# Branch 3 of the dilated attention in whole tiles of q, k, exchanged q and v, loaded two residues ahead, its outputs in one tile of 15 slots, and two weight blocks loaded over a shorter stretch

## The chip, the cores and the metric

One core of a Trainium2 chip runs the whole program. The metric is device time in microseconds, the median of several executions. The core's engines work through queues of their own, in order: PE (TensorE, the matrix products), ACT (ScalarE), DVE (VectorE), POOL (GpSimd) and SP (SyncE), which here issues nearly all transfers (DMAs). An instruction waits on semaphores for what others make; whatever stands behind it on its engine waits with it.

## The reference

The kernel computes one step of a one-layer hybrid decoder on a prompt of 2048 positions and 64 sample rows (8 sequences of 8 new positions on a cache). A normed input is projected once into q, k, v of an attention, qb, kb, vb of a gated linear attention (GLA), its low-rank gate, and two output gates. The attention has three branches of (window, dilation); their outputs are mixed by their softmax denominators. GLA runs over chunks of 64. Both results are gated and go through one output projection:

```
DILATED = ((128, 1), (512, 4), (2048, 16))

def dilated_branch_prompt(q, k, v, window, dil):
    n_keys = window // dil + 1
    lm = S // dil
    ...
    valid = (dist >= 0) & (dist < n_keys) & (key_m >= 0)
    s = jnp.einsum('brnqhd,brnkhd->brnqhk', qr, kk) * (hd ** -0.5)
    s = jnp.where(valid[None, None, :, :, None, :], s, -jnp.inf)
    o, lse = softmax_attend(s, vv, 'brnqhk,brnkhd->brnqhd')
```

Branch 3 has dilation 16: the positions fall into 16 residues of 128 positions each, and each residue is a causal attention of 128 queries on 128 keys, for 8 heads of width 64.

## The kernel before, in words

The program has three parts in time. In the first, up to about 480 us, the projections v, q and k run over 16 row tiles of 128 positions. In the second, up to about 730 us, the attention runs, woven with the projection qkb (qb and kb together). In the third GLA runs, woven with the projections g (gates), vb (value gates) and gb; at the end come the mixing and the output projection (Y, L1658).

**Projections.** `project` (L1107) multiplies in f16 with every number split into a high and a low half: 24 matmuls for one row tile and one block (L1127), with `hr`/`hl` as weights of the array. Their sums are called acc_qkb, acc_g, acc_vb, acc_gb. They need no result of the attention, and so serve as filler between its matmuls. Weights come in through a chain, `load_w`: per block 8 loads from DRAM (`wr_`, L601), a pass of squares on ACT (`jw_`, L622), and a scaling into the two halves on ACT (L649) and DVE (L650).

**Attention.** Branches 1 and 2 run in units (`unit`, L829), then branch 3 (`branch3`, L912): 16 residues r, each in two halves a of four heads, 32 sub-items in all. A sub-item has four stages: `pre` (the loads), `qk` (L444: scores s of high and low halves; DVE adds the mask and takes the row's limit, L452; ACT takes the exponential, L455), `tr` (PE transposes p, L462; ACT with DVE, L424 and L425, or ACT twice and POOL, L427 to L429, split it into halves pt) and `pv` (L477: the output O; ACT and DVE add its halves, L493 and L494; SP stores it, L937). `pipeline` (L1074) staggers them: in one round come qk of sub-item n, pre of n+1, pv of n-3 and tr of n-1.

For the scores, branch 3 needs the query tile twice: as loaded, with the high halves in 64 partitions and the low ones in the other 64, and with the two exchanged. `exchanged` (L815) makes the second with two DVE copies (L818). `turned3` loads the transposed q and k of a residue (L909), one residue ahead; `pre` loads v (L925). Their tiles lie in the pool b3, with two buffers for each of Tq (as loaded and exchanged side by side), Tk and v3. The outputs o lie in the pool op with seven buffers, which the units share.

**Order.** `weave` (L358) interleaves generators: at each point it advances the one whose share done, (steps + 0.5) / declared steps, is smallest. L1218 weaves the rest of qkb, the attention, the weight chain of g and vb (declared 4 x KT = 32 steps, where it has 34 yields) and the sample attention's dots. A scheduler then fixes the order of instructions on each engine from its own estimate of their times; the tile framework adds the waits. A DMA on SP takes one of eight semaphores in turn, DMAHW0 to DMAHW7, and waits for the one issued eight before it.

**GLA.** Its pools (L1224) are opened after the attention's pools are closed, and take over their memory. What lies on a tile's place must have been read, or its store landed, before the new tile is written. Eight cores of 256 positions (`gla_core`, L143) each load zqk and zg (L155, L161), transpose the gates (pg, L190), build decays and scores (sc, L281) and end with the transposes ptk (L324).

Of the kernel before, what the change touches and what calls it, by code (L numbers as in the profile page):

```python
# [7 lines left out]
F32 = mybir.dt.float32  # L8
F32R = mybir.dt.float32r
F16 = mybir.dt.float16  # L10
# [8 lines left out]
P = 128  # L19
D = 1024  # L20
KT = D // P
NH = 8
# [30 lines left out]
def tile_hymba(ctx: ExitStack, tc: tile.TileContext, A: dict):  # L53
    nc = tc.nc
    PE, ACT, DVE, POOL, SP = nc.tensor, nc.scalar, nc.vector, nc.gpsimd, nc.sync
# [20 lines left out]
    o3_d = scratch("o3_d", S, 528)  # L76
# [4 lines left out]
    kp_d = dram.tile([S, 2 * NH * HD], F16, name="kp_d")  # L81
    qp_d = dram.tile([S, 2 * NH * HD], F16, name="qp_d")
    vp_d = dram.tile([S, 2 * NH * HD], F16, name="vp_d")
# [263 lines left out]
    def by16(ap, r):  # L347
        return ap.rearrange("(i r) c -> r i c", r=16)[r]
# [3 lines left out]
    def chain(*gens):  # L352
        for g in gens:
            yield from g
# [3 lines left out]
    def weave(*parts, until=()):  # L358

        until = list(until or parts)
        parts = list(parts)
        for p in parts:
            p.append(0)
        while any(any(q is p for p in parts) for q in until):
            for p in sorted(parts, key=lambda p: (p[2] + 0.5) / p[1]):
                r = next(p[0], parts)
                if r is not WAIT:
                    break  # L370
            p[2] += 1
            if r is parts:
                parts = [q for q in parts if q is not p]
        return [[g, n - done] for g, n, done in parts]
# [7 lines left out]
    with ExitStack() as c1:  # L382
# [22 lines left out]
        op = c_att.enter_context(tc.tile_pool(name="op", bufs=7))  # L405
        ap_ = c_att.enter_context(tc.tile_pool(name="ap", bufs=2))
# [182 lines left out]
        def load_w(name, between=(), behind=()):  # L589

            if name in ("o0", "o1"):
                src, c0, n, rows, sh = w_out, 512 * int(name[1]), 512, nwo, 1.0
            else:
                src, (c0, n), rows, sh = w_in, BLOCKS[name], nw, H_SCALE
            raws = []
            mx = sm.tile([P, KT], F32, name=f"wm_{name}", tag="wm")
            for k in range(KT):
                if k % 2 == 0:
                    pair = wr.tile([P, 2, 528], F32, name=f"wr_{name}_{k}", tag="wr")
                raw = pair[:, k % 2]  # L600
                SP.dma_start(raw[:, :n], src[k * P : (k + 1) * P, c0 : c0 + n])  # L601
                raws.append(raw)
                if k == KT // 2 - 1:
                    for f in between:
                        fetch(f)
            for f in behind:
                fetch(f)


            exact = name == "v"  # L610
            for k in range(KT):
                if exact:
                    DVE.tensor_reduce(
                        mx[:, k : k + 1], raws[k][:, :n], AX.X, ALU.max, apply_absolute_value=True
                    )
                else:
                    tag = {} if name in ("q", "k", "qkb") else {"bufs": 1}
                    jk = zp.tile(
                        [P, 2 * D if tag else D], BF16, name=f"jw_{name}_{k}",
                        tag="z4" if tag else "z1", **tag,  # L620
                    )
                    ACT.activation(  # L622
                        jk[:, :n], raws[k][:, :n], AF.Square, scale=rows[:, k : k + 1],
                        accum_out=mx[:, k : k + 1],
                    )
                yield
            if exact:
                DVE.tensor_tensor(mx[:], mx[:], nwa[:], ALU.mult)
            m1 = sm.tile([P, 1], F32, name=f"w1_{name}", tag="w1")
            DVE.tensor_reduce(m1[:], mx[:], AX.X, ALU.max)  # L630
            pw = kp.tile([P, 1], F32, name=f"pw_{name}")
            DVE.tensor_scalar(
                pw[:], spread_max(m1[:], name), 2.0**-80 if exact else 2.0**-120, None, ALU.max
            )
            if not exact:
                ACT.activation(pw[:], pw[:], AF.Ln)
                ACT.activation(pw[:], pw[:], AF.Exp, scale=0.5)
            power(pw[:], pw[:])
            inv = kp.tile([P, 1], F32, name=f"wi_{name}")
            DVE.tensor_scalar(inv[:], pw[:], 1.0 / (W_SCALE * sh), None, ALU.mult)  # L640
            nws = sm.tile([P, KT], F32, name=f"ns_{name}", tag="ns")
            r = sm.tile([P, 1], F32, name=f"pr_{name}", tag="pr")
            DVE.reciprocal(r[:], pw[:])
            DVE.tensor_scalar(nws[:], rows[:], r[:], W_SCALE, ALU.mult, ALU.mult)
            yield
            w = wp.tile([P, 2, KT, 528], F16, name=f"w_{name}", tag="w")
            for k in range(KT):
                h, l = w[:, 0, k, :n], w[:, 1, k, :n]
                ACT.activation(h, raws[k][:, :n], AF.Copy, scale=nws[:, k : k + 1])  # L649
                DVE.scalar_tensor_tensor(  # L650
                    l, raws[k][:, :n], nws[:, k : k + 1], h, ALU.mult, ALU.subtract
                )
                yield
            loaded[name] = (w, inv)
            powers[name] = pw
# [159 lines left out]
        def exchanged(out, in_):  # L815

            for j in range(2):
                DVE.tensor_copy(out[64 * j : 64 * j + 64], in_[64 - 64 * j : 128 - 64 * j])  # L818
# [83 lines left out]


        T3 = [{} for _ in range(16)]

        def turned3(r):
            for nm_, src, nb in (("q", qp_d, 16), ("k", kp_d, 8)):
                t = b3.tile([P, nb, P], F16, name=f"T3_{nm_}_{r}", tag=f"T{nm_}")
                SP.dma_start_transpose(t[:, 0:8], by16(src, r))  # L909
                T3[r][nm_] = t  # L910

        def branch3(r):  # L912
            T = T3[r]

            def pre():
                if r == 0:
                    turned3(0)
                if r < 15:
                    turned3(r + 1)
                yield  # L920
                exchanged(
                    *(T["q"][:, a : a + 8].rearrange("p h i -> p (h i)") for a in (8, 0))
                )
                T["v"] = b3.tile([P, 1024], F16, name=f"v3_{r}", tag="v3")
                SP.dma_start(T["v"][:], by16(vp_d[:], r))  # L925
                for a in range(2):
                    T["o", a] = op.tile([P, 4, 66], F32, name=f"o3_{r}_{a}", tag="o")

            def OT(a, i):
                if ("O", a) not in T:  # L930
                    T["O", a] = ps_O.tile([P, 512], F32, name=f"O3_{r}_{a}", tag="O")
                return T["O", a][:, i * P : i * P + P]

            def post(a):
                o = T["o", a]
                added(o[:, :, 0:64], T["O", a][:])
                SP.dma_start(  # L937
                    by16(o3_d[:, 264 * a : 264 * a + 264], r), o[:].rearrange("p h d -> p (h d)")
                )

            return [
                attend(
                    f"3_{r}_{a}", 4, 1,
                    lambda i, a=a: [
                        (T["q"][:, 8 * part + 4 * a + i], T["k"][:, 4 * a + i])
                        for part in range(2)
                    ],
                    m3,
                    lambda i, b, a=a: T["v"][:, (4 * a + i) * P : (4 * a + i + 1) * P],
                    lambda i, a=a: T["o", a][:, i, 65:66],  # L950
                    lambda i, a=a: T["o", a][:, i, 64:65],
                    lambda i, a=a: OT(a, i),
                    pre=None if a else pre, post=lambda a=a: post(a), neg=scl["s"][:],
                )
                for a in range(2)
            ]
# [85 lines left out]
        for nm_, src in (("q", A["q_norm_w"]), ("k", A["k_norm_w"])):  # L1042
            i = "qk".index(nm_)
# [24 lines left out]
        kk = ap_.tile([P, NH, 4, 2, P], F16, name="kk", tag="kk", bufs=1)  # L1068
# [3 lines left out]
        work, side = deque(), deque()  # L1072
# [125 lines left out]
        b3 = right(c_b3, "b3", 2)  # L1198
# [12 lines left out]
        def dots():  # L1211
            while side:
                side.popleft()()
                yield

        att = [attention(), 5.2 * len(work)]
        host = [rest("qkb"), steps("qkb")]
        weave(host, att, [chain(load_w("g"), load_w("vb")), 4 * KT], [dots(), len(side) + 3])  # L1218
        c_b3.close()
        c_dot.close()  # L1220
        c_att.close()
# [24 lines left out]
        for lst, nm_, shape, m, eng in (  # L1246
# [3 lines left out]
            for i in range(m):  # L1250
                t = gst.tile(shape, F32, name=f"{nm_}{i}")
# [784 lines left out]
```

## Time and profile before

| | us |
|---|---|
| runs of the kernel before | 1328.85, 1334.85, 1334.49 |
| their median | 1334.49 |
| the profiled execution | 1337.86 |
| its span in the trace | 1336.1 |

The kernel's profile is one execution. Its page gives the busy time of each engine; windows give the same for a stretch, with the clock that was granted to PE (1.00 is full) and the share of time in which the DMA engines were busy. A row of waits names the engine, the instruction that waited, what it waited for, and then the total in us, the number of times and the longest. A row of the chain of waits is a start, a duration and the work or wait that lay on the path. A group of instructions by line ends with its count, its busy time in us, the mean of one in ns and the idle time before them. PEld is the loading of weights into the array, beside PE. The SP queue's rows (SPq) are the issue of a DMA, not its transfer. Rows of PE are modelled at their ends, so that neighbours can overlap by a little.

In the order of instructions, a row is its number, the line, the operation, out<-in with tile and buffer number, and in brackets the engines or DMA semaphores that it waits for.

### The profile page before, as it was taken

The numbers are of one execution on the slowest core, as the hardware profiler recorded it, in microseconds if no ns is written. First come the engines' busy times: TensorE is split into PE (matmuls) and PEld (weight loads), VectorE is DVE, ScalarE is ACT, GpSimd is POOL, SyncE is SP. The second block draws the span as 40 slices with busy tenths as digits, with TensorE's granted clock in tenths as the row PEclk, the third lists the DMA queues.
The fourth block names the chain that finished last, engine by engine and source line by source line (L and its number), as shares of the span: only waits on it lengthen the run. The fifth ranks groups of instructions, "written<-read, shape, count | busy, mean of one in ns | idle before, by whom it ended". The sixth has DMA issues, their size and how long they took to land.

```text
span 1336.1 us, 26268 instructions
## 1 busy us (share of the span) xinstructions
PE 1219.8 (91%) x8910; PEld 732.2 (55%) x8910; DVE 919.4 (69%) x2271; ACT 877.0 (66%) x2332; POOL 631.5 (47%) x596
## 2 busy tenths in 40 slices
PE   3797999989889898998999899999999989999998
PEld 1333565555555555676777566666655445444443
DVE  6357667788767876776765988777672388787741
ACT  5645787777668875878897667665774475565610
POOL 0067545678678745561113965665452144232310
PEclk9989999999999899999899999999999989999999
DMA  8859967777875599969886556553334788998952
GB/s 257 248 152 238 223 198 159 195 209 229 206 201 172 156 265 274 319 218 225 194 210 179 183 165 210 167 167 119 108 101 158 256 253 288 363 344 324 334 194 79
DMA packets 251800, 285.27 MB, mean 214 GB/s; under 512 B 125441, under 2 KB 160338, under 8 KB 251666
## 3 DMA queue, kind: packets, MB, share of 16 engines
q1 hardware_dynamic: 251666, 283.60, 70.7%
q8 instruction: 70, 1.15, 0.4%
q14 instruction: 64, 0.52, 0.1%
HBM read 183.12 MB, written 75.24 MB: 193 GB/s over the span
## 4 chain that ended last, share of the span: by engine, by line
PE 35%; DVE 19%; DMA 16%; issue 11%; ACT 9%; POOL 9%; SPq 2%; POOLq 0%; DVEq 0%; ACTq 0%
PE Y L1658 6%; PE acc_vb L1127 3%; DVE qbd L252 3%; PE acc_gb L1127 3%; PE acc_qkb L1127 3%; PE acc_g L1127 3%; POOL pr L965 2%; PE t L462 2%; PE O L477 2%; DMA T_q<-qp_d 2%; PE s L444 2%; DVE p L452 2%; DVE sck L970 2%; POOL pt L429 2%; DVE ks L249 1%
## 5 line engine op out<-in xcount | busy, mean ns | idle before, releaser
L1127 PEld LDWEIGHTS <-hr 128*128 128x128 f16 x1824 | 174.0, 99 | 133.9 <-issue 16.0
L1127 PEld LDWEIGHTS <-hl 128*128 128x128 f16 x1248 | 122.7, 100 | 154.9 <-issue 28.8
L455 ACT ACTIVATE p<-p,o 128x256 f32<-128x256 f32 (+1 forms) x384 | 173.3, 455 | 47.0 <-DVE o L452 39.8
L1658 PE MATMUL Y<-w_o,mh 128*128 128x512 f16 x768 | 178.0, 383 | 6.7 <-ACT mh L1617 6.6
L965 POOL TENSOR_TENSOR pr<-k,qb 128x512 f32<-128x512 f32 x96 | 132.5, 1380 | 91.8 <-DVE sck L970 58.6
L429 POOL TENSOR_TENSOR pt<-p,pt 128x512 f16<-128x512 f32 (+1 forms) x80 | 94.2, 1178 | 156.3 <-ACT pt L428 125.9
L477 PE MATMUL O<-v,pt 128*128 128x128 f16 x1200 | 113.1, 223 | 22.1 <-POOL pt L429 9.7
L1658 PEld LDWEIGHTS <-mh 128*128 128x128 f16 x768 | 71.9, 98 | 94.3 <-issue 9.0
L970 DVE TENSOR_REDUCE sck<-pr 128x8 f32<-128x512 f32 x128 | 85.6, 678 | 48.9 <-POOL pr L965 48.7
L462 PE MATMUL t<-ident,p 128*128 128x128 f32 x600 | 108.8, 286 | 7.3 <-ACT p L455 5.7
L477 PEld LDWEIGHTS <-pt 128*128 128x128 f16 x1200 | 83.7, 100 | 47.5 <-POOL pt L429 14.3
L1127 PE MATMUL acc_v<-w_v,hl 128*128 128x512 f16 x384 | 96.5, 396 | 8.8 <-DVE vp L759 3.1
L1127 PE MATMUL acc_g<-w_g,hr 128*128 128x272 f16 (+1 forms) x768 | 102.9, 280 | 0.0
L452 DVE CUSTOM_DVE_ANT_0 p<-s,m3w,scl_s 128x128 f32<-128x128 f32 (+1 forms) x256 | 89.0, 394 | 15.9 <-PE s L444 5.7
L1700 POOL TENSOR_TENSOR tc<-oc,w 128x512 f32<-128x512 f32 x32 | 47.0, 1490 | 111.7 <-DVE w L1692 104.8
L1127 PE MATMUL acc_q<-w_q,hl 128*128 128x512 f16 x384 | 93.8, 394 | 4.6 <-ACT zs_k L677 3.8
L244 ACT ACTIVATE E<-D_e 128x256 f32<-128x256 f32 x168 | 66.2, 417 | 43.8 <-POOL D_e L236 26.2
L1127 PE MATMUL acc_k<-w_k,hl 128*128 128x512 f16 x384 | 90.4, 381 | 3.1 <-ACT zs_k L677 2.6
L1127 PE MATMUL acc_vb<-w_vb,hr 128*128 128x512 f16 x384 | 89.1, 379 | 2.3 <-ACT zg L733 2.3
L444 PE MATMUL s<-kk,qq 128*128 128x256 f16 (+1 forms) x512 | 82.4, 273 | 8.9 <-DMA kk<-kp_d 5.2
L1127 PE MATMUL acc_gb<-w_gb,hr 128*128 128x512 f16 x384 | 87.7, 381 | 0.0
L462 PEld LDWEIGHTS t<-ident,p 128*128 128x128 f32 x600 | 70.3, 146 | 18.1 <-ACT p L455 11.3
(509 smaller groups left out, 2630.4 us busy)
## 6 DMA issues: line engine op xcount, KB each, us to landing
k<-in_cache_k_win SPq DMA_DIRECT2D x104, 256.0 KB
sv<-in_cache_v_win SPq DMA_DIRECT2D x24, 1024.0 KB
hr<-h_d SPq DMA_DIRECT2D x44, 512.0 KB
qb<-q_d SPq DMA_DIRECT2D x64, 256.0 KB
o_d<-o SPq DMA_DIRECT2D x96, 132.0 KB
oc<-o_d SPq DMA_DIRECT2D x48, 264.0 KB
x<-in_x_prompt SPq DMA_DIRECT2D x16, 512.0 KB
h_d<-hl SPq DMA_DIRECT2D x16, 512.0 KB
```

The lines of the kernel that those rows point to most:

```text
L244: ACT.activation(ev[rows, i], dv[rows, :, half, :], AF.Exp, scale=(2 * half - 1) / 16.0)
L429: POOL.tensor_tensor(l, f, h, ALU.subtract)
L444: PE.matmul(s_ps[:, i * w : (i + 1) * w], q, k, start=(n == 0), stop=(n == len(prods) - 1),)
L452: DVE.tensor_tensor_reduce(s[:, sl], s_ps[:, sl], mask, neg, BIG, ALU.add, ALU.min, nmf(i))
L455: ACT.activation(s[:, sl], s[:, sl], AF.Exp, bias=nmf(i), scale=-1.0, accum_out=denf(i))
L462: PE.transpose(p_ps[:, i * P : (i + 1) * P], t["s"][:, i * P : (i + 1) * P], ident[:])
L477: PE.matmul(o_, t["pt"][:, c, (i * nb + b) * P : (i * nb + b + 1) * P], vf(i, b), start=(n == 0), stop=(n == 2 * nb - 1),)
L965: POOL.tensor_tensor(pr[:], kt, qt, ALU.mult)
L970: DVE.tensor_reduce(out, pr[:].rearrange("p (u k d) -> p u k d", u=2, k=4), AX.X, ALU.add)
L1127: PE.matmul(z, a_[:, k, :], w[:, p_, k, cols], start=(k == 0 and i == 0), stop=(k == KT - 1 and i == 2),)
L1658: PE.matmul(Y[:], a_[:, k, :], w_[:, part, k, :512], start=(i == 0), stop=(i == len(prods) - 1),)
L1700: eng.tensor_tensor(t_[:], oc[:, g, :, 0:64], w[:, g].unsqueeze(2).to_broadcast([P, NH, HD]), ALU.mult,)
```

## The change

The tiles of branch 3 are now whole: one tile T of four parts holds q, k, the exchanged q (x) and v of a residue. There are four of them: residues with r % 4 below 2 use two buffers of the pool b3, the other two the buffers "qq" of the pool ap_, which the query tiles of branches 1 and 2 had. `turned3` is called two residues ahead instead of one (0, 1 and 2 at the start, then r+2 in the `pre` of r). The load of v goes into the same tile, so that it needs no buffer of its own; the whole tile is free for the next residue when the value products of the one before are done.

The outputs go into one tile out3 of 15 slots, taken in turn by the sub-items, in the place "kk" of ap_ that held the keys of branches 1 and 2. The pool op serves the units alone.

The chain of weights of g and vb is declared 6 x KT = 48 steps in the weave.

```
         T3 = [{} for _ in range(16)]
+        out3 = []
 
         def turned3(r):
-            for nm_, src, nb in (("q", qp_d, 16), ("k", kp_d, 8)):
-                t = b3.tile([P, nb, P], F16, name=f"T3_{nm_}_{r}", tag=f"T{nm_}")
-                SP.dma_start_transpose(t[:, 0:8], by16(src, r))
-                T3[r][nm_] = t
+            pool, tag = (b3, "T") if r % 4 < 2 else (ap_, "qq")
+            t = pool.tile([P, 4, NH, P], F16, name=f"T3_{r}", tag=tag)
+            for i, src in enumerate((qp_d, kp_d)):
+                SP.dma_start_transpose(t[:, i], by16(src, r))
+            T3[r].update(q=t[:, 0], k=t[:, 1], x=t[:, 2], v=t[:, 3])
...
             def pre():
                 if r == 0:
+                    out3.append(ap_.tile([P, 15, 4, 66], F32, name="out3", tag="kk", bufs=1))
                     turned3(0)
-                if r < 15:
-                    turned3(r + 1)
+                    turned3(1)
+                if r + 2 < 16:
+                    turned3(r + 2)
                 yield
-                exchanged(
-                    *(T["q"][:, a : a + 8].rearrange("p h i -> p (h i)") for a in (8, 0))
-                )
-                T["v"] = b3.tile([P, 1024], F16, name=f"v3_{r}", tag="v3")
-                SP.dma_start(T["v"][:], by16(vp_d[:], r))
+                exchanged(*(T[n_].rearrange("p h i -> p (h i)") for n_ in "xq"))
+                SP.dma_start(T["v"].rearrange("p h i -> p (h i)"), by16(vp_d[:], r))
                 for a in range(2):
-                    T["o", a] = op.tile([P, 4, 66], F32, name=f"o3_{r}_{a}", tag="o")
+                    T["o", a] = out3[0][:, (2 * r + a) % 15]
...
-        weave(host, att, [chain(load_w("g"), load_w("vb")), 4 * KT], [dots(), len(side) + 3])
+        weave(host, att, [chain(load_w("g"), load_w("vb")), 6 * KT], [dots(), len(side) + 3])
```

In the changed kernel the loads of T stand in L911, that of v in L926 and the store in L938; the lines behind `branch3` keep their numbers.

More of the change, by code (lines that the diff above doesn't have):

```diff
@@ L937, in post @@
                 SP.dma_start(
-                    by16(o3_d[:, 264 * a : 264 * a + 264], r), o[:].rearrange("p h d -> p (h d)")
+                    by16(o3_d[:, 264 * a : 264 * a + 264], r), o.rearrange("p h d -> p (h d)")
                 )
@@ L944, in branch3 @@
                     lambda i, a=a: [
-                        (T["q"][:, 8 * part + 4 * a + i], T["k"][:, 4 * a + i])
-                        for part in range(2)
+                        (T[n_][:, 4 * a + i], T["k"][:, 4 * a + i]) for n_ in "qx"
                     ],
                     m3,
-                    lambda i, b, a=a: T["v"][:, (4 * a + i) * P : (4 * a + i + 1) * P],
+                    lambda i, b, a=a: T["v"][:, 4 * a + i],
                     lambda i, a=a: T["o", a][:, i, 65:66],
```

## The prediction, as it was made

> **What bounds the kernel now.** I read the page first, then the windows of the stretch that the change touches, then the waits and the chain of that stretch. The page says that the whole program is bound by TensorE:
>
> ```profile
> span 1336.1 us, 26268 instructions
> PE 1219.8 (91%) x8910; PEld 732.2 (55%) x8910; DVE 919.4 (69%) x2271; ACT 877.0 (66%) x2332; POOL 631.5 (47%) x596
> ```
>
> So a wait is worth time only where PE is idle. The attention's branch 3 runs from its first score matmul to its last output matmul, in the timeline of PE:
>
> ```profile
> 603.33 0.33 PE L444 MATMUL s<-T_k,T_q 128*128 128x128 f16 x3
> ...
> 728.62 0.61 PE L477 MATMUL O<-v,pt 128*128 128x128 f16 x8
> ```
>
> That is 126 us. The window over it gives the busy time of PE, PEld, DVE, ACT and POOL, then the granted clock:
>
> ```profile
> 600.00:730.00 130.00, 120.28 (x1122) 91.98 (x1120) 83.17 (x364) 111.14 (x402) 23.46 (x22) 0.96 0.81 201
> 630.00:640.00 10.00, 6.01 (x47) 5.60 (x45) 6.45 (x28) 6.87 (x28) 0.00 (x0) 0.69 0.80 176
> 640.00:650.00 10.00, 8.67 (x64) 5.94 (x63) 9.86 (x39) 9.83 (x27) 1.92 (x2) 0.80 0.78 152
> ```
>
> PE is idle for 130 - 120.28 = 9.7 us of it, and the clock of 0.96 costs another 0.04 x 130 = 5.2 us; over half of both lies in the 20 us from 630. What the engines wait for there:
>
> ```profile
> DVE T_q L818 <- DMA T_q<-qp_d: 22.9, 11, 3.9
> DVE o L494 <- ACT ol L493: 13.1, 11, 3.2
> ...
> DVE p L452 <- DMA o_d<-o: 4.2, 4, 1.9
> ```
>
> The first is VectorE, in line for the exchanged copy of a query tile that hasn't landed; the last is VectorE waiting for an output slot whose store hasn't landed. The chain of waits puts both on the path, and with them the scaling of the weights of the value gates (w_vb), which sits in the middle of branch 3:
>
> ```profile
> 626.54 5.64 DMA T_q<-qp_d
> ...
> 643.20 2.56 ACT w_vb L649 x4
> ...
> 699.47 3.24 DMA o_d<-o
> ```
>
> **Branch 3 itself.** The tiles get one sub-item more of lead. Before, the load for residue r+1 could start once the scores of r-1 were done, two of the 32 sub-items ahead of its exchange; now that for r+2 starts after the value products of r-2, which read the v in the same tile, three ahead. A sub-item lasts 126 / 32 = 3.9 us, the longest wait was 3.9 us, so nearly all of the 22.9 us go. With 15 output slots the 4.2 us go too. w_vb moves out, as SyncE's and ScalarE's orders show. On ScalarE, in before, its eight scalings stand between the exponentials of residue 5 (p_5_0, p_5_1):
>
> ```order
> 864 L427 ACTIVATE p_4_1_8211<-t_4_1_8323 128x512 [waits PE_49]
> 865 L649 ACTIVATE w_vb<-wr_vb_7385,ns_vb 128x512 [waits DVE_49]
> 866 L649 ACTIVATE w_vb<-wr_vb_7385,ns_vb 128x512
> 867 L649 ACTIVATE w_vb<-wr_vb_7388,ns_vb 128x512 x2
> 868 L649 ACTIVATE w_vb<-wr_vb_7391,ns_vb 128x512 x2
> 869 L649 ACTIVATE w_vb<-wr_vb_7394,ns_vb 128x512 x2
> 870 L455 ACTIVATE p_5_0_8287,o_5_0_8257<-p_5_0_8287,o_5_0_8257 128x128 [waits DMAHW0_49,DVE_49]
> ```
>
> They take 5.0 us of ScalarE and 6.4 of VectorE:
>
> ```profile
> L649 ACT ACTIVATE w_vb<-wr_vb,ns_vb 128x512 f16<-128x512 f32 x8 | 5.0, 711 | 0.0
> L650 DVE SCALAR_TENSOR_TENSOR w_vb<-wr_vb,ns_vb,w_vb 128x512 f16<-128x512 f32 x8 | 6.4, 847 | 0.0
> ```
>
> In the changed kernel they stand among the last units of branch 2, whose names have four numbers (p_3_1_1_1):
>
> ```order
> 781 L729 ACTIVATE zq_8249<-acc_qkb_8079,wi_qkb 128x512 [waits DMAHW5_49,PE_49]
> 782 L455 ACTIVATE p_3_1_1_1_7476,o_3_1_1_7401<-p_3_1_1_1_7476,o_3_1_1_7401 128x256 [waits DVE_49] x2
> 783 L649 ACTIVATE w_vb<-wr_vb_6908,ns_vb 128x512 [waits DVE_49]
> 784 L649 ACTIVATE w_vb<-wr_vb_6908,ns_vb 128x512
> 785 L649 ACTIVATE w_vb<-wr_vb_6911,ns_vb 128x512 x2
> ```
>
> There PE has projection work to run through, and the engines have room:
>
> ```profile
> 580.00:600.00 20.00, 20.00 (x166) 14.26 (x165) 13.71 (x42) 15.19 (x45) 13.87 (x12) 1.00 0.67 211
> ```
>
> So the block is free there; without that cover it would cost up to 6.4 us. What branch 3 gains lies between two bounds. The lower is PE's idle time, 9.7 us. The upper is ScalarE, late next: 130 - 111.14 + 5.0 = 23.9 us until it is full. In between lies idle time plus clock, 9.7 + 5.2 = 14.9. I take the middle, -17 us.
>
> The clock follows the hole in these rows: 0.69 and 0.80 where PE had 6.01 and 8.67 us of 10, 1.00 in the row at 580, where it had all. The Trainium skill, "TensorE: Matmul & The Clock Gate", Part 1, says that the clock is halved after an idle window of about 3.4 us and returns after as long a busy one; by that rule a closed hole returns its clock in full, and the 5.2 us would come on top of the 9.7. The rows agree in kind; how long a hole must be they don't show.
>
> **Projection work that moves.** PE's order holds the fillers at other places. Ahead of branch 3's first score matmul stand 335 of acc_qkb's 384 matmuls before, 374 now, 39 more. At its last output matmul stand 206 of acc_g and 96 of acc_vb before, 246 and 120 now. Their spacing:
>
> ```profile
> 729.06 3.29 PE L1127 MATMUL acc_g<-w_g,hr 128*128 128x272 f16 x28
> ...
> 734.43 4.06 PE L1127 MATMUL acc_vb<-w_vb,hr 128*128 128x512 f16 x18
> ```
>
> 3.29 / 28 = 0.118 us for acc_g, 4.06 / 18 = 0.226 for the 512 wide ones, acc_qkb among them. All qkb matmuls are done by the end of branch 3 in both, so up to that end PE has 40 x 0.118 + 24 x 0.226 = +10.1 us more to do. Branch 3 ends at -17 + 10.1 = -6.9 us.
>
> **The start of the linear attention (GLA).** Its tiles lie in before where nothing of branch 3 lies, and its first loads are issued before branch 3 begins:
>
> ```profile
> 600.71 0.90 SPq L155 DMA_DIRECT2D zqk_e<-zqk_d  x2
> ```
>
> SyncE's order in before, at the last branch 2 stores (L874) and the first loads of GLA (L155):
>
> ```order
> 543 L874 DMA o_d<-o_3_1_3_7176 128x264 [waits DMAHW1_49,DVE_49]
> 544 L874 DMA o_d<-o_3_1_0_7261 128x264 [waits DMAHW2_49,DVE_49]
> 545 L155 DMA zqk_e_9831<-zqk_d 128x2x512 [waits DMAHW3_49,PE_49]
> 546 L155 DMA zqk_e_10052<-zqk_d 128x2x512 [waits DMAHW4_49]
> 547 L976 DMA sc_d<-sck_7617 128x128 [waits DMAHW5_49,DVE_49]
> ```
>
> Now the space is taken by the tiles and outputs of branch 3, and the same loads stand behind its last store (L938, row 676), waiting for the stores' landing:
>
> ```order
> 673 L938 DMA o_d<-out_7673 128x264 [waits DMAHW3_49,DVE_49]
> 674 L567 DMA hr_10111<-h_d 128x2048 [waits DMAHW4_49,PE_49]
> 675 L747 DMA vb_d<-vbs_10106 128x512 [waits DMAHW5_49,Activation_49]
> 676 L938 DMA o_d<-out_7673 128x264 [waits DMAHW6_49,DVE_49]
> 677 L155 DMA zqk_e_9768<-zqk_d 128x2x512 [waits DMAHW6_49,DMAHW7_49,DMAHW3_49,DMAHW1_49]
> 678 L161 DMA zg_e_9770<-zg_d 128x2x16 [waits DMAHW0_49]
> ```
>
> Some 130 rows later, with branch 3 over. Behind row 677 queue all further loads, and GpSimd, PE and VectorE wait for this one. PE has filler in the meantime: from the last output matmul to GLA's first scores (sc) 67 acc_g and 24 acc_vb before, 97 and 48 now, that is 13.3 and 22.2 us: +8.9 us. In PE's order the row tile of acc_g ahead of sc has gone from 5 to 7. Before:
>
> ```order
> 8565 L1127 MATMUL acc_g_5_10263<-w_g,hr_9725 128x256
> 8566 L1127 LDWEIGHTS hr_9725
> 8567 L1127 MATMUL acc_g_5_10263<-w_g,hr_9725 128x256
> 8568 L281 MATMUL sc_e_1_10005<-qbd_9450,ks_9444 64x64 [waits DVE_49]
> ```
>
> And now:
>
> ```order
> 8804 L1127 MATMUL acc_g_7_10555<-w_g,hr_9905 128x272
> 8805 L1127 LDWEIGHTS hr_9905
> 8806 L1127 MATMUL acc_g_7_10555<-w_g,hr_9905 128x272
> 8807 L281 MATMUL sc_e_1_9942<-qbd_9387,ks_9381 64x64 [waits DVE_49]
> ```
>
> GLA's first scores come at 744.57 in before; the transposes ptk mark the end of each of its eight cores, the first four here:
>
> ```profile
> 744.57 0.63 PE L281 MATMUL sc_e<-qbd,ks 128*64 128x64 f32 x14
> 759.80 0.38 PE L324 MATMUL ptk_e<-ident,kd_e 128*128 128x128 f32 x2
> 795.21 0.38 PE L324 MATMUL ptk_e<-ident,kd_e 128*128 128x128 f32 x2
> 833.28 0.38 PE L324 MATMUL ptk_e<-ident,kd_e 128*128 128x128 f32 x2
> 867.95 0.49 PE L324 MATMUL ptk_e<-ident,kd_e 128*128 128x128 f32 x3
> 740.00:840.00 100.00, 91.30 (x824) 63.44 (x822) 89.74 (x127) 66.91 (x172) 74.78 (x61) 0.98 0.58 184
> ```
>
> The scores will come at -6.9 + 8.9 = +2 us. PE then has 10.1 + 8.9 = 19 us more of projections behind it, and from the third core's ptk on its order is that of before again, so the first three cores run with 19 us less between their matmuls. But VectorE is busy for 89.74 of the 100 us from 740: they can gain at most its 10.3 idle us, and nothing if their chain is paced by VectorE and GpSimd alone. I take the middle, -5 us, which would bring the spacings of 35.4 and 38.1 us down to those of 34.7 that follow. After that nothing differs, and the shift stays to the end.
>
> **The weights' loads.** Declaring the chain of loads 48 steps long instead of 32, while it has 34, lets each step come earlier: wr_vb's eight loads move in SyncE's queue from the stretch around 546 into that before 540:
>
> ```profile
> 500.00:540.00 40.00, 35.41 (x247) 22.45 (x246) 26.14 (x75) 21.97 (x65) 19.79 (x16) 0.91 0.98 273
> 540.00:560.00 20.00, 20.00 (x141) 12.35 (x139) 16.44 (x33) 17.88 (x45) 12.05 (x9) 1.00 1.00 345
> ...
> 545.97 5.61 DMA wr_vb<-in_w_in
> ...
> wr_vb<-in_w_in SPq DMA_DIRECT2D x8, 256.0 KB
> ```
>
> The DMA share is 0.98 there and 1.00 here, but PE is idle for 4.6 us there and for none here. Eight times 256 KB at 345 GB/s are 6.1 us, the upper bound; the load's own 5.61 us on the chain, gone, is the lower. I take 0, as the transfers only change places. The Trainium skill, "DMA: Bandwidth & Descriptors", under Issuing engines are not separate DMA queues, says that all transfers run on the same 16 engines and interleave. By that rule what waits in the earlier stretch, GpSimd's keys and the transposed tiles, pays nearly the whole 6.1 us, and the sum would be +3; the shares agree with it, but whether PE's path pays is not in them.
>
> **The sum.** -17 (branch 3) + 10.1 (fillers ahead) + 8.9 (start of GLA) - 5 (its first cores) + 0 (loads) = -3 us. Reckoned against the profiled execution, 1337.86 us with a span of 1336.1, that gives 1334.9; this execution is 3.4 us above the median of the runs, 1334.49, so on the median it is 1331.5 us.
>
> **The rivals.** *The gain comes through in full* (faster). Branch 3 shrinks until ScalarE is full, -23.9, and the first GLA cores take all of VectorE's idle time, -10.3: with + 10.1 + 8.9 that is -15.2 us, 1319.3. For it: the T_q and slot waits add up to 27.1 us, more than ScalarE's slack. Against it: the chain in branch 3 also has exponentials and output sums (13.1 us of VectorE on ol) that the change leaves alone.
>
> *The start of GLA costs more than its filler covers* (slower). The first loads stand behind the last stores. In before the path from the first transpose of gates to the first scores is 744.57 - 725.48 = 19.1 us:
>
> ```profile
> 725.48 0.38 PE L190 MATMUL pg_e<-ident,zg_e 128*16 128x128 f32 x2
> ...
> 730.13 0.35 SPq L937 DMA_DIRECT2D o_d<-o  x1
> ```
>
> The last store is issued 1.25 us behind the last output matmul (730.48 - 729.23). With a store's landing (3.24 us on the chain) and a load like T_q's (5.64) the first scores come 1.25 + 3.24 + 5.64 + 19.1 = 29.2 us behind that matmul, against 15.3 before: +13.9 instead of +8.9. If the cores then keep their spacing, the sum is -17 + 10.1 + 13.9 = +7 us, 1341.5. It decides if the scores come over 25 us behind branch 3's end. For it: VectorE's 90%. Against it: part of those 19.1 us was waiting for VectorE's other work, since nothing was in a hurry.
>
> *The change doesn't do what it says.* Each T load still queues on SyncE behind stores that wait for VectorE, and the slot is freed by a later step than before; if the tiles land no earlier, only the slots and w_vb are won, 4.2 + 2.6 (w_vb's piece on the chain) = 6.8 instead of 17: +7.2, 1341.7 too. Against it is the count of sub-items above; it would show as VectorE's wait on T unchanged.
>
> **How the numbers follow.** About 0.5%, 6.7 us, is what a measurement of this kernel can tell from no change. The forecast (1331.5, own range -11 to +5 by the bounds of the terms) has a chance of 0.50, of which 0.13 lies beyond -6.7 and 0.02 beyond +6.7. The full gain has 0.22, all of it faster; the late GLA 0.20, 0.14 of it slower; the unchanged wait 0.08, 0.06 of it slower. Faster is 0.13 + 0.22 = 0.35, slower 0.02 + 0.14 + 0.06 = 0.22, no change the other 0.43. The range goes from 1319, where the full gain stands, to 1345, half of the 6.1 us of the loads above the slower rivals.
>
> **What would show it.** Right: VectorE's wait for T under 5 us; the window from 600 on with PE full and its clock at 1.00 until branch 3's end at about 722; first sc at 745 to 748; ptk's first spacings near 35. Wrong: T waits that stay; PE idle between the last output matmul and the first sc; or, on the fast side, branch 3 over by 715.

## The result and the profile after

The changed kernel takes 1344.32 us in the median of 14 runs (1340.07 to 1351.36), the kernel before 1334.34 (14 runs): the ratio is 1.0084, with a 95% interval of 1.0066 to 1.0103. It is slower by 0.84%, about 11 us. The forecast was 3 us faster. Its profiled execution took 1344.58 us, 6.7 more than that of before (1337.86); single executions of one kernel scatter by several us (those of the kernel before lie between 1328.85 and 1346.16), so the sums below explain the 6.7 of the two traces, and the verdicts rest on the timed ratios.

The page of the changed kernel, span and PE's row:

```profile
span 1342.8 us, 26248 instructions
PE 1215.0 (90%) x8910; PEld 728.3 (54%) x8910; DVE 925.3 (69%) x2271; ACT 876.7 (65%) x2332; POOL 633.8 (47%) x596
```

Branch 3 from its first scores to its last output matmuls, then GLA's first scores, in the timeline of PE:

```profile
609.48 0.33 PE L444 MATMUL s<-T 128*128 128x128 f16 x3
...
730.17 0.55 PE L477 MATMUL O<-T,pt 128*128 128x128 f16 x7
...
757.19 0.63 PE L281 MATMUL sc_e<-qbd,ks 128*64 128x64 f32 x14
...
774.33 0.60 PE L324 MATMUL ptk_e<-ident,kd_e 128*128 128x128 f32 x4
...
797.82 0.63 PE L324 MATMUL ptk_e<-ident,kd_e 128*128 128x128 f32 x4
...
838.73 0.66 PE L324 MATMUL ptk_e<-ident,kd_e 128*128 128x128 f32 x4
...
874.83 0.60 PE L324 MATMUL ptk_e<-ident,kd_e 128*128 128x128 f32 x4
```

Branch 3 takes 121 us (126 before), but it begins 6.2 us later, and ends 1.5 us later instead of 6.9 earlier. GLA's first scores come 26.5 us behind the last output matmul (15.3 before), 12.6 us later than before. At the ptk that end the first four cores the delay is 14.5, 2.6, 5.4 and 6.9 us; from there on the cores keep the spacing of before. The windows of the two stretches, and of ten us in branch 3 (busy PE, PEld, DVE, ACT, POOL, then the clock):

```profile
600.00:730.00 130.00, 121.45 (x1167) 92.71 (x1165) 81.56 (x355) 108.23 (x398) 24.97 (x23) 0.99 0.74 189
740.00:840.00 100.00, 83.78 (x736) 59.59 (x736) 87.12 (x123) 65.38 (x170) 73.25 (x60) 0.91 0.56 177
680.00:690.00 10.00, 6.67 (x49) 3.74 (x47) 4.76 (x23) 4.89 (x19) 0.85 (x1) 0.83 0.88 204
```

PE's idle time from 600 to 730 is 8.6 us, where 9.7 stood before; of the two losses named in the forecast only the clock's has gone (0.99 instead of 0.96), but for a new hole from 680 to 690. From 740 to 840 PE now idles for 16.2 us, before for 8.7: it has run ahead of time some of the projections that used to stand there. The waits say why branch 3 gained so little:

```profile
DVE T L818 <- DMA T<-qp_d: 25.4, 13, 3.9
DVE out L494 <- ACT ol L493: 13.9, 10, 3.7
```

No wait for an output slot is left, but VectorE waits for T as long as before (25.4 us; 22.9). The chain of waits of the changed kernel shows the start of GLA as the second rival had it, last store, then load, then GLA's own steps:

```profile
731.62 6.45 DMA o_d<-out
738.65 3.23 DMA zg_e<-zg_d
742.31 0.44 PE ptg_e L195 x4
...
751.46 2.04 POOL D_e L236 x2
```

The store took 6.45 us to land and not 3.2, and the load stands right behind its landing. The reason for the T waits lies in one residue, here the ninth (r = 8), in the timeline of the changed kernel:

```profile
655.47 0.61 PE L477 MATMUL O<-T,pt 128*128 128x128 f16 x8 [1.68 <-ACT p L427]
...
656.10 1.38 SPq L911 DMA_TRANSPOSE T<-qp_d  x1
...
660.59 0.98 DVE L818 COPY T<-T 64x1024 f16<-64x1024 f16 x2 [1.97 <-DMA T<-qp_d]
...
661.84 0.33 PE L444 MATMUL s<-T 128*128 128x128 f16 x3
```

The load is issued as soon as the value products of r = 4 have released the slot, and its scores follow 5.7 us later, directly behind landing and exchange. It is so throughout: in the changed kernel the loads of residues 4 to 15 go out 0 to 4.5 us behind the last value product of the residue whose slot they take; in the kernel before they go out 0 to 2.1 us behind the last scores of the residue two ahead of them. In the kernel before, for the eighth residue (r = 7):

```profile
637.32 1.23 SPq L909 DMA_TRANSPOSE T_q<-qp_d  x1
...
640.99 0.85 DVE L818 COPY T_q<-T_q 64x1024 f16<-64x1024 f16 x2
...
650.09 0.61 PE L444 MATMUL s<-T_k,T_q 128*128 128x128 f16 x8
```

There the load comes 12.8 us ahead of its use, the longest lead of these residues, and the finished copy waits 8.2 us for PE. So "two residues ahead" in the code is later on the chip. Issue to first use over residues 4 to 15, as the traces have them: 7.3 to 12.8 us before, with a mean of 9.6; 5.1 to 10.8 in the changed kernel, with a mean of 7.0, and under 7 us for seven of the twelve.

### The profile page after: what moved, and what is told of

It reads as the page before. It is cut to its first block, busy times and chain, and to the rows that moved or that the text cites. A ratio compares the mean times of both kernels' runs of the same rounds, so it can differ in the third digit from the quotient of the medians.

```text
span 1342.8 us, 26248 instructions
## 1 busy us (share of the span) xinstructions
PE 1215.0 (90%) x8910; PEld 728.3 (54%) x8910; DVE 925.3 (69%) x2271; ACT 876.7 (65%) x2332; POOL 633.8 (47%) x596
## 4 chain that ended last, share of the span: by engine, by line
PE 33%; DVE 21%; DMA 17%; issue 10%; ACT 8%; POOL 7%; SPq 3%; DVEq 0%; POOLq 0%; ACTq 0%
PE Y L1658 6%; PE acc_gb L1127 4%; DVE qbd L252 3%; PE acc_vb L1127 2%; PE acc_qkb L1127 2%; PE O L477 2%; DMA T<-qp_d 2%; PE acc_g L1127 2%; PE s L444 2%; PE acc_q L1127 2%; PE t L462 2%; DMA v<-vp_d 2%; DVE sck L970 2%; DVE p L452 2%; POOL pr L965 2%
## 5 line engine op out<-in xcount | busy, mean ns | idle before, releaser
L455 ACT ACTIVATE p<-p,o 128x256 f32<-128x256 f32 (+1 forms) x256 | 123.3, 484 | 42.0 <-DVE o L452 39.6
L477 PE MATMUL O<-v,pt 128*128 128x128 f16 x944 | 88.2, 220 | 20.6 <-POOL pt L429 7.2
L244 ACT ACTIVATE E<-D_e 128x256 f32<-128x256 f32 (+1 forms) x168 | 66.1, 417 | 44.2 <-POOL D_e L236 22.9
L444 PE MATMUL s<-kk,qq 128*128 128x256 f16 (+1 forms) x512 | 81.6, 270 | 13.9 <-DVE o L452 7.3
L1127 PE MATMUL acc_vb<-w_vb,hr 128*128 128x512 f16 x384 | 93.4, 384 | 0.0
L236 POOL TENSOR_TENSOR D_e<-b_e 128x512 f32<-128x512 f32 x56 | 70.0, 1261 | 19.7 <-DVE b_e L223 14.7
```

The lines of the kernel that those rows point to most:

```text
L236: dec = POOL.tensor_tensor(dv, bv, bv[:, :, 0:1, B - 1 : B].to_broadcast([P, M, 2, B]), ALU.subtract)
L244: ACT.activation(ev[rows, i], dv[rows, :, half, :], AF.Exp, scale=(2 * half - 1) / 16.0)
L444: PE.matmul(s_ps[:, i * w : (i + 1) * w], q, k, start=(n == 0), stop=(n == len(prods) - 1),)
L455: ACT.activation(s[:, sl], s[:, sl], AF.Exp, bias=nmf(i), scale=-1.0, accum_out=denf(i))
L477: PE.matmul(o_, t["pt"][:, c, (i * nb + b) * P : (i * nb + b + 1) * P], vf(i, b), start=(n == 0), stop=(n == 2 * nb - 1),)
L1127: PE.matmul(z, a_[:, k, :], w[:, p_, k, cols], start=(k == 0 and i == 0), stop=(k == KT - 1 and i == 2),)
```

## The experiments

Four theories stood against each other. **A**: GLA's late start is the loss. **B**: the earlier weights are. **C**: the exchanged copy waits merely because it stands in VectorE's queue where the scheduler took the load to land. **L**, stated only after e1 to e4: v inside the tile keeps the slot until the value products, so that the loads come too late. All times are ratios to the kernel before on the same chip; positions are those of each run's trace, us from its start. Branch 3 goes from its first score matmul to the end of its last output matmul; the last column is the ptk that ends GLA's fourth core.

| run | ratio (95%) | branch 3 begins | takes | first scores of GLA behind its end | at | fourth ptk |
|---|---|---|---|---|---|---|
| before | 1 | 603.3 | 125.9 | 15.3 | 744.6 | 868.0 |
| changed | 1.0084 (1.0066 to 1.0103) | 609.5 | 121.2 | 26.5 | 757.2 | 874.8 |
| e1 chain 32 | 1.0049 (1.0029 to 1.0070) | 600.9 | 126.1 | 23.1 | 750.1 | 871.9 |
| e2 chain 48 alone | 0.9991 (0.9968 to 1.0014) | 607.6 | 113.7 | 17.5 | 738.8 | 863.3 |
| e3 GLA early | 1.0056 (1.0032 to 1.0080) | 612.0 | 120.5 | 17.8 | 750.3 | 873.3 |
| e4 late exchange | 1.0051 (1.0033 to 1.0070) | 612.6 | 121.1 | 24.7 | 758.3 | 874.4 |
| e5 v apart | 1.0014 (0.9994 to 1.0033) | 617.4 | 111.5 | 25.3 | 754.2 | 872.2 |
| e6 three repairs | 0.9981 (0.9960 to 1.0001) | 609.4 | 116.9 | 16.0 | 742.3 | 865.1 |
| e7 15 slots alone | 1.0032 (1.0010 to 1.0053) | 599.3 | 125.0 | 23.5 | 747.8 | 870.4 |
| e8 before again | single execution | 601.7 | 126.9 | 15.3 | 744.0 | 867.9 |
| e9 lead alone | 1.0002 (0.9982 to 1.0023) | 600.7 | 123.7 | 15.3 | 739.8 | 863.8 |
| e10 all, no costs | 0.9998 (0.9978 to 1.0018) | 612.7 | 116.4 | 17.6 | 746.6 | 869.0 |
| e11 same, late exchange | 1.0010 (0.9985 to 1.0035) | 609.7 | 113.7 | 19.5 | 742.8 | 865.3 |
| e12 lead with v inside | 1.0079 (1.0048 to 1.0110) | 600.0 | 130.0 | 17.3 | 747.3 | 876.7 |

**e1, the weights undone.**

```
-        weave(host, att, [chain(load_w("g"), load_w("vb")), 6 * KT], [dots(), len(side) + 3])
+        weave(host, att, [chain(load_w("g"), load_w("vb")), 4 * KT], [dots(), len(side) + 3])
```

> The changed kernel with the weight chain declared 32 steps again; tiles and output slots as changed. If the late start of GLA costs the time (theory A: its first loads stand behind the last stores of branch 3), the first scores still come 24 to 28 us behind the last output matmul and the time stays within 4 us of the changed kernel's, 1340 to 1348 us. If the earlier weight loads cost it (theory B: they go into a stretch where the transfers are full, and 39 more qkb matmuls stand ahead of branch 3), the time falls back to 1331 to 1337. VectorE's wait for T stays at 20 to 28 us by theory C (the exchanged copy stands in VectorE's queue where the scheduler took the load to land, so more lead in SyncE's queue changes nothing).

1.0049 lies between the two expectations: the time falls by 0.35%, and over half of the loss stays. The first scores come 23.1 us behind branch 3, and VectorE waits 19.5 us for T, both just under the ranges of A and C.

**e2, the weights alone on the kernel before.** The same line, the other way round.

> The kernel before with the weight chain declared 48 steps and nothing else. Theory A: within 4 us of the kernel before, 1331 to 1339, the first scores 14 to 18 us behind the last output matmul. Theory B: 1340 or more, with PE's idle time between 500 and 600 up by 3 us or more.

0.9991: the earlier weights alone cost nothing that can be measured, so B falls. They don't help in the end either, though branch 3 shrinks from 125.9 to 113.7 us. Freed from w_vb, it begins 4.3 us later, behind 39 more qkb matmuls.

**e3, GLA's loads freed.** The waits of a reused place go by whole pools here: when branch 3 uses a tile of the pool ap_, GLA's first loads move behind branch 3 in SyncE's order (e7 shows it for one tile alone). So the two extra tiles get a pool of their own at the same addresses, and the outputs go back to op.

```
+        aq = c_att.enter_context(tc.tile_pool(name="aq", bufs=2))
...
-            pool, tag = (b3, "T") if r % 4 < 2 else (ap_, "qq")
+            pool, tag = (b3, "T") if r % 4 < 2 else (aq, "qq")
...
-                    T["o", a] = out3[0][:, (2 * r + a) % 15]
+                    T["o", a] = op.tile([P, 4, 66], F32, name=f"o3_{r}_{a}", tag="o")[:]
```

> The changed kernel, but the two extra tiles lie in a pool of their own at the same addresses, and the outputs lie in the seven buffers of before, so that the first loads of GLA need not wait for branch 3. Theory A: first scores 14 to 18 us behind the last output matmul instead of 26.7, and the time 7 to 12 us below the changed kernel's, 1332 to 1338. Theory B: at most 3 us below it, 1341 to 1347. Theory C: VectorE's wait for T still 20 to 28 us, so no gain on the kernel before.

The gap falls to 17.8 us as it should, the time by 0.28% only, which the two intervals don't tell from nothing. A is right about the gap and wrong about the size: the loss is mostly elsewhere.

**e4, the exchanged copy forced late.** x leaves the tile for two half tiles of one buffer each.

```
+                for a in range(2):
+                    x = T["x", a] = b3.tile([P, 4, P], F16, name=f"X3_{r}_{a}", tag=f"x{a}", bufs=1)
+                    exchanged(*(
+                        t.rearrange("p h i -> p (h i)")
+                        for t in (x[:], T["q"][:, 4 * a : 4 * a + 4])
+                    ))
```

> The changed kernel with the exchanged copy in two half tiles of one buffer each, so that a copy can't be placed ahead of the scores of the residue before, some 4 us before its use, when the load has long landed. Theory C: VectorE's wait for T under 6 us instead of 25.4, branch 3 from first score to last output matmul 110 to 116 us instead of 121, and the time 4 to 10 us below the changed kernel's. If the wait only covered other waits (rival: branch 3 is held by ScalarE and the output sums), the wait goes and branch 3 stays within 3 us of 121, the time within 3 us of 1344.

C fails here. Even so placed, the copy finds the tile not landed, and branch 3 takes 121.1 us. In VectorE's waits of this run, with x now named X:

```profile
DVE X L818 <- DMA T<-qp_d: 16.4, 10, 2.5
```

The time falls by 0.33% all the same, which no theory had for this reason.

**e5, v apart.**

```
-            t = pool.tile([P, 4, NH, P], F16, name=f"T3_{r}", tag=tag)
+            t = pool.tile([P, 3, NH, P], F16, name=f"T3_{r}", tag=tag)
...
+                T["v"] = b3.tile([P, NH, P], F16, name=f"v3_{r}", tag="v3")
```

> The changed kernel with v in two buffers of its own, as before, so that a tile of q, k and exchanged q is free after the scores instead of after the value products. In the changed kernel a tile's load was issued only about 6 us ahead of its use (in the kernel before 8 to 12 us). Lead theory (L): with v apart the load is issued over 15 us ahead of its use, VectorE's wait for T falls under 6 us, branch 3 (first score to last output matmul) under 115 us from 121, and the time 5 to 10 us below the changed kernel's, 1334 to 1339. Queue theory (C): the exchanged copy moves ahead in VectorE's queue together with the load, to where the scheduler takes the load to land, so VectorE still waits 15 to 28 us for T and branch 3 takes 117 to 122 us; the time 1340 to 1345. The late start of GLA stays in both: first scores 22 to 27 us behind the last output matmul.

The time falls to 1.0014, 0.7% below the changed kernel, with GLA still late (25.3 us). The loads of residues 4 to 15 now come 19 to 26 us ahead of their use. Window and wait of this run:

```profile
600.00:730.00 130.00, 126.25 (x1216) 96.72 (x1214) 89.47 (x369) 115.15 (x414) 29.17 (x25) 1.00 0.75 195
```

```profile
DVE T L818 <- DMA T<-qp_d: 14.8, 11, 2.9
```

PE idles for 3.8 us instead of 8.6, though VectorE still waits 14.8 us for T. L has the time, and C comes close with the waits but not with time and length: the copy stands in VectorE's queue ahead of the load's landing, and there it costs little as long as the scores come much later (14 to 22 us behind the copy in this run). That the scheduler's estimate put it there is not shown.

**e6, three repairs together**: v apart, the copy late, GLA's loads freed.

> Three repairs together: v apart, the exchanged copy in two half tiles of one buffer each so that it can't stand far ahead of its use, and GLA's first loads freed from branch 3 (the extra tiles in a pool of their own, outputs in the seven buffers of before); weight chain 48 steps. All theories: VectorE's wait for T under 4 us, first scores 14 to 18 us behind the last output matmul. If these are what the change lost (theories A with C or L), branch 3 takes 108 to 115 us and the time is 1322 to 1331, at or below the kernel before. If branch 3 is held by other waits (rival: the ScalarE and VectorE steps between scores and output), it takes 117 us or more and the time is 1333 to 1339.

At 1331.86 us and 0.9981 (0.9960 to 1.0001) this is the fastest version, clear of the changed kernel, and not clear of the kernel before. Time and branch 3 (116.9 us) lie between the two expectations. T waits are gone; with seven output buffers VectorE waits for slots instead:

```profile
DVE p L453 <- DMA o_d<-o: 10.3, 10, 2.4
```

**e7, the 15 slots alone** on the kernel before (out3 in the place "kk", all else as before).

> The kernel before with only its outputs of branch 3 put into the 15 slots in the place of the keys; tiles and weight chain as before. Theory A (the late GLA): first scores 22 to 28 us behind the last output matmul instead of 15.4, VectorE's 4 us of waits for output slots gone, and the time 4 to 9 us above the kernel before. If the late start is made up in full by the first GLA cores (rival), the time is within 2 us of the kernel before.

1.0032, 4.3 us: the late GLA alone costs about half of its 8 us of gap, though the waits for output slots are gone here too.

**e8, the kernel before once more.**

> The kernel before once more, for its profile: how far one profiled execution differs from another. Expected: span 1329 to 1337 us, branch 3 within 6 us of 125.7, the first scores 15 to 17 us behind it.

Span 1337.4 us, just above what was expected, with every position of the table within 1.6 us of the first trace. Its time, 1339.14, lies 4.8 us above the median of the runs of the kernel before on this chip (1334.39), the first one's 3.5. So positions of two such traces can be compared to 2 us, and whole times are better taken from the timed runs.

**e9, the lead alone**: four tiles of q, k and x two residues ahead, v apart, outputs in op, chain 32, GLA's loads free.

> The kernel before with the loads of q and k two residues ahead in four tiles (the two extra ones in a pool of their own), v apart as before, outputs in the seven buffers, weight chain 32 steps, GLA's loads early: the lead alone. If the lead of the tiles is worth something by itself, PE's idle time from 600 to 730 falls from 9.7 us by 3 us or more, branch 3 takes 113 to 120 us and the time is 3 to 8 us below the kernel before. If VectorE's waits for tiles and slots cost nothing that PE's projections don't cover anyway (rival), the time is within 2 us of the kernel before, branch 3 over 121 us.

1.0002, with branch 3 at 123.7 us: the rival's case. Nothing is gained in time. For the eleventh residue (r = 10) the timeline of this run has the load 25 us ahead of the scores:

```profile
645.11 1.26 SPq L912 DMA_TRANSPOSE T<-qp_d  x1
...
649.16 0.86 DVE L819 COPY T<-T 64x1024 f16<-64x1024 f16 x2
...
670.36 0.61 PE L445 MATMUL s<-T 128*128 128x128 f16 x8
```

And still, window and wait are nearly those of the kernel before:

```profile
600.00:730.00 130.00, 121.36 (x1136) 93.30 (x1135) 83.60 (x362) 110.25 (x401) 25.47 (x25) 0.97 0.81 203
```

```profile
DVE T L819 <- DMA T<-qp_d: 21.7, 10, 3.2
```

**e10, all that the change wanted without its two costs**: e9 with chain 48 and 14 output slots in the place of the units' v tiles, whose pool is closed at the third residue.

> All that the change wanted, without its two costs: tiles of q, k and exchanged q two ahead in four slots, v apart, 14 output slots in the place of the units' v tiles (free when branch 3 has begun), weight chain 48 steps, GLA's loads early. Expected: no wait for output slots, VectorE's wait for T about 15 us but far ahead of the use, branch 3 110 to 115 us, first scores 15 to 18 us behind it, the time 1324 to 1331, 4 to 10 us below the kernel before. If branch 3's gain is eaten by its later start and by the first GLA cores (rival), 1331 to 1335.

0.9998, the rival's case. Branch 3 is 9.5 us shorter and begins 9.4 us later; the first scores come at 746.6, 2 us later than before. VectorE waits 23.6 us for T, and not 15. Its windows:

```profile
600.00:730.00 130.00, 122.49 (x1180) 94.13 (x1179) 84.20 (x360) 111.48 (x409) 28.64 (x25) 0.99 0.80 202
740.00:840.00 100.00, 86.77 (x768) 59.06 (x766) 90.42 (x128) 65.70 (x169) 73.40 (x61) 0.95 0.55 177
```

What PE idles less in the first window (7.5 us, before 9.7) it idles more in the second (13.2, before 8.7), where VectorE is busy for 90.4 of 100 us.

**e11, e10 with the copy late.**

> The same with the exchanged copy in two half tiles of one buffer each, so that VectorE does not wait for T at all. If those 15 us of waits cost anything once the loads have lead, the time is 2 to 5 us below the same kernel without the half tiles; if not, within 2 us of it, or above by the two more copies per residue (32 x about 0.3 us of VectorE, off PE's path).

1.0010. VectorE waits for T no more, its largest wait in branch 3 is that for the output sums:

```profile
DVE out L496 <- ACT ol L495: 14.9, 10, 4.0
```

```profile
600.00:730.00 130.00, 126.23 (x1233) 98.56 (x1231) 97.47 (x401) 112.55 (x411) 27.30 (x27) 1.00 0.84 211
```

PE idles for 3.8 us of the 130, and the time doesn't move.

**e12, e9 with v inside the tile**, that one difference.

```
-            t = pool.tile([P, 3, NH, P], F16, name=f"T3_{r}", tag=tag)
+            t = pool.tile([P, 4, NH, P], F16, name=f"T3_{r}", tag=tag)
...
-                T["v"] = b3.tile([P, NH, P], F16, name=f"v3_{r}", tag="v3")
```

> The same as the run of the lead alone (four tiles, the extra ones in a pool of their own, outputs in seven buffers, weight chain 32 steps, GLA's loads early), but with v inside the tile as in the change: this one difference. Theory L (a tile with v is free only after the value products, so its next load comes late): loads issued only 5 to 8 us ahead of the first use instead of 15 to 35, the scores right behind the exchanged copy, branch 3 124 to 130 us instead of 123.5, the time 4 to 9 us above the kernel before. If v inside costs only together with the early weights or the late GLA (rival), the time is within 2 us of the kernel before and branch 3 within 2 us of 123.5.

1.0079: this one difference brings back nearly the whole loss, with GLA early, weights as before and seven output buffers. The same residue (r = 10) in its timeline:

```profile
669.10 1.23 SPq L912 DMA_TRANSPOSE T<-qp_d  x1
...
673.03 0.86 DVE L819 COPY T<-T 64x1024 f16<-64x1024 f16 x2 [0.95 <-DMA T<-qp_d]
674.19 0.49 PE L445 MATMUL s<-T 128*128 128x128 f16 x6
```

5.1 us from issue to use, where e9 has 25. In its window PE idles for 13.0 us where e9 has 8.6:

```profile
600.00:730.00 130.00, 116.98 (x1094) 89.07 (x1093) 79.64 (x351) 107.36 (x389) 21.47 (x19) 0.96 0.78 197
```

The loss doesn't all arise in branch 3. This trace is 5.6 us behind that of e9 at the end of branch 3, 7.5 at GLA's first scores, and 12.9 at the fourth core's ptk. Why the delay more than doubles behind branch 3 is not shown.

## Why the prediction was wrong

**The lead (failed).** "Three ahead" was counted in rounds of the pipeline as the code states them. The slot comes free when the engine has run the value products, and on the chip these lag behind the scores of their own residue by more: the load of r = 8, which takes the slot of r = 4, went out at 656.1, 23 us behind the first scores of r = 4 at 632.7, where four rounds of the forecast's 3.9 us would be 16. In the kernel before, the scores alone freed the tile of q. So the load moved later, not earlier, and the next scores follow right behind it. PE's own waits for such a load are short (0.2 us in all in the changed kernel, 1.9 in e12); most of its waits name VectorE, in whose queue the copy stands. e12 against e9 shows what putting v inside costs, 0.8%; how it costs this is shown in branch 3 (5.6 of the 12.9 us between their traces) and open behind it. That VectorE's wait would stay was the third rival, with a chance of 0.08; it had the sign and the wait (25.4 us), for the reason that its slot is freed by a later step.

**The price of the waits (failed).** The forecast took waits of VectorE, 22.9 us for T and 4.2 for slots, and PE's 9.7 us of idle time as time to be won. e9 has the lead and e11 removes every wait for T, and both stand within 0.2% of the kernel before. A wait in VectorE's queue was counted as if it were on PE's path; in the kernel before the scores come 1.6 to 8.2 us after the exchanged copy in all of those twelve residues. By the forecast's own sum the -17 us came out as -8.6: branch 3 ended 1.5 us later, with 10.1 us more of projections ahead of that end. And where branch 3 did get 9.5 us and more shorter (e2, e5, e10, e11), the time didn't follow: it begins later with the longer chain (by 4 to 14 us in these traces), and PE idles more in the first GLA cores (busy for 91.3 of 100 us before, 84.6 in e2, 86.8 in e10, 84.3 in e11). That VectorE paces those cores fits its 87 to 96 busy us of the same 100 in these runs, but no run tests it. The clearest case is e2: the longer chain alone, with w_vb out of branch 3, ends it 7.9 us earlier with 5.6 us more of projections ahead (32 matmuls of acc_g, 8 of acc_vb), -13.5 by the same sum, and the time stays.

**Fillers ahead.** Right: in the traces too, 40 more matmuls of acc_g and 24 of acc_vb stand ahead of branch 3's end, the forecast's +10.1. Ahead of its first scores stand 39 more of acc_qkb, 8.8 us, of which 6.2 showed as a later start.

**The start of GLA.** +8.9 was forecast by PE's fillers, 13.9 by the rival's chain; the gap grew by 11.1. The second rival had the mechanism: PE idles for 1.75 us in that gap, behind the store and the load. The first cores were to give back 5: the shift is 12.6 us at the first scores and 6.9 at the fourth core (867.95 before, 874.83 now), 5.7 given back. The sum is near, the course isn't: the spacings that were to come near 35 measured 23.5, 40.9 and 36.1, so that the delay fell to 2.6 us at the second core and grew again; why is open. By the positions, -8.6 + 10.1 + 11.1 - 5.7 = +6.9 us, against the 6.7 between the two profiled executions.

**The weights' loads.** 0 was taken, and e2 measures 0.9991. In the changed kernel, though, undoing them is worth 0.35% (e1): the parts don't add up. The 15 slots alone cost 0.32%, v inside 0.79%, both together with the longer chain 0.84%. Why less than the sum stays open. That the timed medians differ by 10 us and the traces by 6.7 comes from the executions that were profiled: that of before lay 3.5 us above its median (its second one, e8, 4.8), that of the changed kernel 0.3.

The granted clock behaved as forecast: 0.96 with the hole in branch 3, 1.00 from 600 to 730 in e5 and e11, where PE idles for 3.8 us, 0.83 in the new hole of the changed kernel, and 0.91 in its window from 740, where PE now idles. In the Trainium skill, "TensorE: Matmul & The Clock Gate", Part 1, idle stretches lower the clock and busy ones bring it back. The rows agree; but the clock that came back bought no time here (e10, e11), since PE idled later instead.

## What to carry to other kernels

Before widening a tile, ask which reader frees it last: a part with a later reader (v, read by the value products) ties the slots of all other parts to it, and "two ahead" in the code can be later in time. Measure the lead from issue to first use in the trace, and price a wait by what its engine's followers have to do with the bound engine, not by its length. And ask who inherits the memory: a place that was free early may be what lets the next stage load in advance.

## What the runs showed of the hardware

The landing of a store is not a constant: the last one of 132 KB took 6.45 us in the changed kernel, and two on the chain of the kernel before took 3.24 and 3.72 us. Why is not shown; the DMA engines were busy for a share of 0.61 over the long one and of 0.89 and 0.74 over the short ones. In the changed kernel the load that waited for the store paid all of it, ahead of its own 3.2 us.
